# Two-block transformer on one core: gate and up of the feed-forward stages in seven products of quadrants instead of eight, down in five passes laid between the units

## The chip, the core and the metric

The kernel runs on one core of a Trainium2 chip. The metric is the device time of one execution in microseconds; the kernel before has a median of 3131.32 us over three runs (3129.34 to 3133.84).

Engines: TensorE (PE, matmuls; PEld its weight loads), VectorE (DVE), ScalarE (ACT), GpSimd (POOL), and SyncE (SP), which here issues the DMAs.

## The reference

512 tokens of width 1024 pass through one attention block (three attention branches, a linear recurrence, an output projection, a feed-forward stage) and then two layers of feed-forward stage, mixing stage (four kinds of attention over quarters of the width), feed-forward stage and final norm. A feed-forward stage is

```python
D_FF = -(-8 * D_MODEL // 768) * 256          # 2816

def rms_norm(x, g):
    y = xf * lax.rsqrt(jnp.mean(xf * xf, axis=-1, keepdims=True) + EPS)
    return (y * g.astype(jnp.float32)).astype(x.dtype)

def swiglu(h, w_gate, w_up, w_down):
    return (jax.nn.silu(h @ w_gate) * (h @ w_up)) @ w_down
```

so five times in the program: h = norm(x); x = x + c * swiglu(h), with c = 1 in stage 0 and 0.5 in stages 1 to 4. In order: attention block, output projection, stage 0, stage 1, mixing, stage 2, final norm, stage 3, mixing, stage 4, final norm.

## The kernel before, in words

Activations lie transposed: 8 tiles of 128 (width) by 512 (tokens). Every factor of a product is split in a high and a low part of the reduced type fp32r, and a product is three matmuls, high x high, low x high and high x low (`feat`, L142 to L144).

*Weights.* `stream` loads a block in pieces of 128x1024 (512 KB, L118, two buffers "raw" that all stages share), ScalarE makes the high part (L125) and VectorE or GpSimd the low part (L127), in halves of 512.

*A feed-forward stage* (`ffn`). Eleven units: each streams two weight blocks (gate, up; 8 k-tiles by 256 columns), multiplies them into two banks of 128x512 each, scales by the norm's broadcast factor rB (L521, L527), applies Silu (L522), multiplies (L528) and splits the result in fh and fl (L211 on ScalarE, L212 on VectorE). Then down: four blocks of 22 k-tiles, each adding two finished tiles into xT (L537, L539).

*Norm.* The factor of a token, 1/sqrt(mean x^2), is applied behind the matmul, so the next stage's matmuls need only xh and xl, the tile times the norm's gain. For each finished tile of xT, `norm_sq` squares it on ScalarE (L223) and sums on GpSimd (L225), and `norm_split` makes xh (L229, ScalarE) and xl (L230, VectorE). When all eight are done, `norm_r` reduces over partitions on PE (L195, `tokred`), makes the power (L186 VectorE, L188 GpSimd), and broadcasts on PE (L204, `bcast`) with a copy on ScalarE to rB (L207). `final_norm` does this with a second sum and also scales all of xT (L610).

*Order.* Instructions are put in order per engine by a scheduler, by priority: a `high_priority` block with a larger offset is drawn further ahead. Each engine runs its own queue in that order and waits on semaphores. Buffers come from pools; a pool closed at the end of a stage gives its memory to the pool opened next.

Of the kernel before, what the change touches and what calls it, by code (L numbers as in the profile page):

```python
# [84 lines left out]
class Kern:  # L85
# [419 lines left out]
    def ffn(self, f, half, norm):  # L505

        tc, nc, I = self.tc, self.nc, self.I
        V, S, G = nc.vector, nc.scalar, nc.gpsimd
        xh, xl, rB, xT = self.xh, self.xl, self.rB, self.xT
        ks = [(k, k) for k in range(8)]  # L510
        with tc.tile_pool(name="ph_f", bufs=1) as pf:
            self.pf = pf
            fh = [pf.tile([128, n, T], FR, name=f"fh{i}") for i, n in enumerate((8, 8, 6))]
            fl = [pf.tile([128, n, T], FR, name=f"fl{i}") for i, n in enumerate((8, 8, 6))]
            for j in range(11):
                wg = self.stream(I["w_g"][f, j], 8, 256)
                wu = self.stream(I["w_u"][f, j], 8, 256)
                z = [pf.tile([128, T], FT, tag="z", name="z", bufs=3) for m in range(2)]
                ps = self.feat2(wg, ks, lambda k: xh[:, k], lambda k: xl[:, k])
                for m in range(2):  # L520
                    V.tensor_mul(z[m], ps[m], rB)  # L521
                    S.activation(z[m], z[m], AF.Silu)  # L522
                ps = self.feat2(wu, ks, lambda k: xh[:, k], lambda k: xl[:, k])
                for m in range(2):
                    k = 2 * j + m
                    u = pf.tile([128, T], FT, tag="u", name="u", bufs=2)
                    V.tensor_mul(u, ps[m], rB)  # L527
                    V.tensor_mul(u, u, z[m])  # L528
                    self.split(fh[k // 8][:, k % 8], fl[k // 8][:, k % 8], u)
            for j in range(4):  # L530
                w = self.stream(I["w_d"][f, j], 22, 256)
                ps = self.feat2(w, [(k, k) for k in range(22)], lambda k: fh[k // 8][:, k % 8],
                                lambda k: fl[k // 8][:, k % 8])
                for m in range(2):
                    k = 2 * j + m
                    if half is None:
                        V.tensor_add(xT[:, k], ps[m], xT[:, k])  # L537
                    else:
                        V.scalar_tensor_tensor(xT[:, k], ps[m], half, xT[:, k], op0=OP.mult, op1=OP.add)  # L539
                    norm[0](k)  # L540
# [21 lines left out]
    def final_norm(self, l):  # L562
# [12 lines left out]
        def tile_done(k):  # L575
# [15 lines left out]
            g = gg[:, k:k + 1]  # L591
            S.activation(xh[:, k, :], xk, AF.Copy, scale=g)
            V.scalar_tensor_tensor(xl[:, k, :], xk, g, xh[:, k, :].bitcast(FT), op0=OP.mult, op1=OP.subtract)

        def finish():
            rf = self.rstd(self.tokred(acc, self.ones, 1), 1024, 4, "rt")
            if not last:
# [6 lines left out]
                self.xh, self.xl = xh, xl  # L604
            rB = self.bcast(rf, self.pf, "rF")
# [10 lines left out]
    def mix(self, px, l, norm):  # L616
# [253 lines left out]
        def diff():  # L870
# [29 lines left out]
            def head(h):  # L900
# [31 lines left out]
                def soft(qb):  # L932
# [4 lines left out]
                    for m in range(2):  # L937
# [88 lines left out]
        def na():  # L1026
# [26 lines left out]
            def head(h):  # L1053
# [21 lines left out]
                def soft(cb):  # L1075
# [584 lines left out]
def host(inputs):  # L1660
# [94 lines left out]
    for i, n in enumerate(("w_g", "w_u", "w_d")):  # L1755
        A[n] = np.stack([blocks(f[i], 256) for f in ff])
# [55 lines left out]
```

## Time and profile before

| | |
|---|---|
| median of three runs | 3131.32 us |
| the profiled execution | 3131.08 us, span 3129.3 us, mean granted clock 0.986 |
| PE busy | 3026.2 us, 97%, 15289 matmuls |
| VectorE, ScalarE, GpSimd busy | 55%, 44%, 24% |
| DMA over the span | 88 GB/s |

A window row gives for a stretch the busy time of an engine with the count of its instructions, the clock that was granted to PE (1.00 is 2.4 GHz, 0.50 is 1.2 GHz) and what the DMAs moved. Durations of matmuls overlap, so the step from one start to the next is the cost of one. In a timeline row the bracket at the end is the idle time of the engine before the instruction and what ended it.

### The profile page before, as it was taken

How to read it: one execution, taken by the hardware profiler on the slowest of the kernel's cores; microseconds unless marked ns; L12 is line 12 of the kernel's file. 1: busy time of each engine (PE TensorE's matmuls, PEld its weight loads, DVE VectorE, ACT ScalarE, POOL GpSimd, SP SyncE). 2: the span in 40 equal slices, each digit the busy share in tenths (PEclk: the TensorE clock that was granted, in tenths of full speed). 3: DMA queues.
4: the chain of work that ended last, by engine and by line, in shares of the span. 5: the costliest groups of instructions: out<-in, count | busy, mean ns of one | idle time of the engine just before them, and what ended most of it. 6: DMA issues, size and time to landing. Idle time of an engine off the chain costs nothing.

```text
span 3129.3 us, 41188 instructions
## 1 busy us (share of the span) xinstructions
PE 3026.2 (97%) x15289; PEld 2544.2 (81%) x15289; DVE 1718.7 (55%) x3144; ACT 1390.1 (44%) x2707; POOL 763.6 (24%) x722
## 2 busy tenths in 40 slices
PE   7999999999999999999989999999999998999998
PEld 6888777878888888889877888888888987778886
DVE  7676775444444444336787544355443488665433
ACT  4577774233333333236675333333332577543322
POOL 3466640010000000028863000010000878210000
PEclk9999999999999999999999999999999998999998
DMA  4211112343333233333211333323333321123332
GB/s 143 96 60 60 55 35 77 112 130 95 95 98 98 95 100 96 95 111 107 72 38 41 101 95 99 98 88 98 99 95 97 111 89 47 41 88 94 96 100 81
DMA packets 105266, 275.82 MB, mean 88 GB/s; under 512 B 27172, under 2 KB 36900, under 8 KB 104904
## 3 DMA queue, kind: packets, MB, share of 16 engines
q1 hardware_dynamic: 105064, 273.18, 28.3%
q8 instruction: 120, 1.97, 0.3%
q14 instruction: 82, 0.67, 0.1%
HBM read 268.93 MB, written 6.80 MB: 88 GB/s over the span
## 4 chain that ended last, share of the span: by engine, by line
PE 71%; issue 13%; DVE 7%; POOL 4%; ACT 2%; DMA 1%; SPq 0%; DVEq 0%; POOLq 0%; ACTq 0%
PE ps_mm L142 8%; PE ps_mm L144 8%; PE ps_mm L143 8%; PE ps_s L143 6%; PE ps_s L144 6%; PE ps_s L142 6%; PE ps_t L144 6%; PE ps_t L143 6%; PE ps_t L142 6%; PE ps_mm L172 2%; PE ps_mm L173 2%; PE ps_mm L174 2%; POOL lo L127 1%; PE ps_t L1579 1%; DVE PTl L212 1%
## 5 line engine op out<-in xcount | busy, mean ns | idle before, releaser
L125 ACT ACTIVATE hi<-raw 128x512 fp32r<-128x512 f32 (+2 forms) x952 | 593.7, 626 | 1353.2 <-PE ps_s L143 406.2
L127 DVE TENSOR_TENSOR lo<-raw,hi 128x512 fp32r<-128x512 f32 x782 | 547.5, 702 | 931.3 <-ACT hi L125 920.5
L225 POOL TENSOR_TENSOR acc<-acc,sq 128x512 f32<-128x512 f32 x49 | 74.4, 1518 | 1052.0 <-issue 525.7
L142 PE MATMUL ps_mm<-xh,hi 128*128 128x512 f32 (+1 forms) x792 | 311.2, 393 | 2.6 <-ACT hi L125 2.2
L144 PE MATMUL ps_mm<-xh,lo 128*128 128x512 f32 (+1 forms) x792 | 309.6, 392 | 3.1 <-POOL lo L127 3.1
L143 PE MATMUL ps_mm<-xl,hi 128*128 128x512 f32 (+1 forms) x792 | 310.0, 391 | 0.0
L142 PE MATMUL ps_s<-xh,hi 128*128 128x512 f32 x656 | 253.2, 391 | 7.9 <-ACT hi L125 7.8
L143 PE MATMUL ps_s<-xl,hi 128*128 128x512 f32 x656 | 257.5, 393 | 3.4 <-DVE xl L230 2.9
L172 PE MATMUL ps_mm<-hi,xh 128*128 128x256 f32 (+1 forms) x896 | 255.1, 288 | 2.3 <-ACT tk L651 1.0
L144 PE MATMUL ps_s<-xh,lo 128*128 128x512 f32 x656 | 256.2, 391 | 0.0
L127 POOL TENSOR_TENSOR lo<-raw,hi 128x512 fp32r<-128x512 f32 (+2 forms) x170 | 226.8, 1342 | 117.3 <-ACT hi L125 111.8
L173 PE MATMUL ps_mm<-lo,xh 128*128 128x256 f32 (+1 forms) x896 | 254.5, 286 | 0.1
L174 PE MATMUL ps_mm<-hi,xl 128*128 128x256 f32 (+1 forms) x896 | 252.6, 285 | 0.1
L142 PE MATMUL ps_t<-xh,hi 128*128 128x512 f32 x608 | 237.1, 390 | 0.0
L143 PE MATMUL ps_t<-xl,hi 128*128 128x512 f32 x608 | 236.9, 390 | 0.0
L144 PE MATMUL ps_t<-xh,lo 128*128 128x512 f32 x608 | 236.2, 390 | 0.6 <-DVE lo L127 0.5
L144 PEld LDWEIGHTS ps_mm<-xh,lo 128*128 128x128 f32 (+1 forms) x792 | 148.6, 188 | 35.3 <-POOL lo L127 4.1
L142 PEld LDWEIGHTS ps_mm<-xh,hi 128*128 128x128 f32 (+1 forms) x792 | 148.7, 188 | 34.3 <-ACT hi L125 2.5
L172 PEld LDWEIGHTS ps_mm<-hi,xh 128*128 128x128 f32 x896 | 171.1, 192 | 4.9 <-ACT tk L651 1.3
L173 PEld LDWEIGHTS ps_mm<-lo,xh 128*128 128x128 f32 x896 | 171.9, 192 | 2.2 <-POOL lo L127 0.7
L143 PEld LDWEIGHTS ps_mm<-xl,hi 128*128 128x128 f32 (+1 forms) x792 | 148.8, 188 | 30.5
L174 PEld LDWEIGHTS ps_mm<-hi,xl 128*128 128x128 f32 x896 | 171.2, 192 | 1.9 <-DVE xl L230 0.5
(527 smaller groups left out, 6654.9 us busy)
## 6 DMA issues: line engine op xcount, KB each, us to landing
raw<-in_w_g SPq DMA_DIRECT2D x110, 512.0 KB
raw<-in_w_u SPq DMA_DIRECT2D x110, 512.0 KB
raw<-in_w_d SPq DMA_DIRECT2D x108, 512.0 KB
raw<-in_w_o SPq DMA_DIRECT2D x24, 512.0 KB
raw<-in_w_c SPq DMA_DIRECT2D x16, 512.0 KB
raw<-in_w_m SPq DMA_DIRECT2D x16, 512.0 KB
raw<-in_w_a SPq DMA_DIRECT2D x12, 512.0 KB
raw<-in_w_d SPq DMA_DIRECT2D x20, 256.0 KB
```

The source lines that it names most:

```text
L125: nc.scalar.activation(hi[:, :c], x, AF.Copy)
L127: eng.tensor_tensor(lo[:, :c], x, hi[:, :c].bitcast(FT), op=OP.subtract)
L142: mm(ps, wh, mh(km), start=s, stop=False)
L143: mm(ps, wh, ml(km), start=False, stop=False)
L144: mm(ps, wl, mh(km), start=False, stop=e)
L172: mm(out[tb], h, wh, start=k == 0 and tb % 2 == 0, stop=False)
L173: mm(out[tb], h, wl, start=False, stop=False)
L174: mm(out[tb], o, wh, start=False, stop=k == K - 1 and tb % 2 == 1)
L212: self.nc.vector.tensor_sub(lo, src, hi.bitcast(FT))
L225: nc.gpsimd.tensor_tensor(acc, acc, sq, op=OP.add)
L1579: PE.transpose(tps[:, (qb - kb) * 128:(qb - kb + 1) * 128], P[qb][:, kb * 128:kb * 128 + 128], ident)
```

## The change

Gate and up of a unit form a matrix of two by two quadrants (k-tiles even and odd; gate and up) and the activations one of two by two (k-tiles even and odd; tokens 0 to 255 and 256 to 511). Seven products of sums of quadrants take the place of eight (Winograd's form of Strassen's scheme). `combine` makes from each finished pair of tiles of x the seven right factors, split in high and low; in a unit, GpSimd makes four sums of weight tiles (L571), ScalarE and VectorE split seven weight tiles of 128x1024 (L578, L579), PE runs seven products of 24 matmuls of 256 columns, and VectorE, ScalarE and GpSimd add the seven results up to gate and up (L619 to L647) ahead of the scaling and Silu in `act` (L596 to L598). Down runs in five passes over 4, 4, 4, 4 and 6 k-tiles; the first four lie between products of units 2, 4, 6, 8 and later ones, each pass adding into xT (L668). The weights of gate and up lie in a new order in the inputs, four tiles A0 to A3 of 128x1024 per unit; A0, A2, A3 come into four buffers "raw2" of the stage's own pool, A1 into the shared "raw". The mixing stage has some tiles moved into the memory that holds the combinations otherwise.

```diff
+    def combine(self, k, xk, g, xc):
+        V, S = self.nc.vector, self.nc.scalar
+        p = k // 2
+        if k % 2 == 0:
+            xc["x"] = self.t4("x")
+            if "hi" not in xc:
+                xc["hi"], xc["lo"] = ((self.xp.tile([128, 4, 4, 256], FR, tag="x" + n, name="x" + n),
+                                       self.x3.tile([128, 4, 3, 256], FR, tag="x3" + n, name="x3" + n)) for n in "hl")
+        x = xc["x"]
+        hi, lo = xc["hi"], xc["lo"]
+        S.activation(x[:, 2 * (k % 2):2 * (k % 2) + 2], xk.rearrange("p (a b) -> p a b", a=2), AF.Copy, scale=g)
+        if k % 2 == 0:
+            self.split(hi[0][:, p, 0], lo[0][:, p, 0], x[:, 0])
+            return
+        self.split(hi[0][:, p, 1:3], lo[0][:, p, 1:3], x[:, 2:4])
+        t = self.t4("t")
+        V.tensor_sub(t[:, 0], x[:, 1], x[:, 0])
+        V.tensor_sub(t[:, 1], x[:, 3], t[:, 0])
+        V.tensor_sub(t[:, 2], x[:, 3], x[:, 1])
+        V.tensor_sub(t[:, 3], x[:, 2], t[:, 1])
+        self.split(hi[0][:, p, 3], lo[0][:, p, 3], t[:, 0])
+        self.split(hi[1][:, p], lo[1][:, p], t[:, 1:4])
+    def norm_c(self, gname, g0):
+        acc, xc, xT = self.new_acc(), {}, self.xT
+        def tile_done(k):
+            self.combine(k, xT[:, k], self.col(gname, g0 + k), xc)
+            self.norm_sq(xT[:, k], k, acc)
+        def finish():
+            self.xc = xc["hi"], xc["lo"]
             self.r, self.rB = self.norm_r(acc)
         return tile_done, finish
...
@@ -504,40 +545,151 @@
     def ffn(self, f, half, norm):
         tc, nc, I = self.tc, self.nc, self.I
...
+        V, S, G, mm = nc.vector, nc.scalar, nc.gpsimd, nc.tensor.matmul
+        rB, xT = self.rB, self.xT
         with tc.tile_pool(name="ph_f", bufs=1) as pf:
             self.pf = pf
...
+            self.t4 = lambda n: pf.tile([128, 4, 256], FT, tag="c", name=n, bufs=3)
+            xh, xl = ([lambda p, c=c, x=x: x[c // 4][:, p, c % 4] for c in range(7)] for x in self.xc)
+            rT = rB.rearrange("p (t b) -> p t b", t=2)[:, :, None, :].to_broadcast([128, 2, 2, 256])
+            fh, fl = {}, {}
+            nbank = [0]
+            def load(u, i):
+                pool, tag, n = (self.wp, "raw", 2) if i == 1 else (pf, "raw2", 4)
+                t = pool.tile([128, 2 * T], FT, tag=tag, name=f"A{i}", bufs=n)
+                with tc.high_priority(offset=6000):
+                    nc.sync.dma_start(t, I["w_gu"][f, u, i])
+                return t
+            def add(a, b, op=OP.subtract):
+                t = pf.tile([128, 2 * T], FT, tag="S", name="S", bufs=3)
+                with tc.high_priority(offset=3000):
+                    G.tensor_tensor(t, a, b, op=op)
+                return t
+            def prod(x, c, ranges=((0, 4),)):
+                h, o = (pf.tile([128, 2 * T], FR, tag=n, name=n, bufs=3) for n in ("wh", "wl"))
+                with tc.high_priority(offset=3000):
+                    S.activation(h, x, AF.Copy)
+                    V.tensor_sub(o, x, h.bitcast(FT))
+                nbank[0] += 1
+                ps = self.bank(("mm", "s")[nbank[0] % 2])
+                for a, b in ranges:
+                    for i in range(2):
+                        out = ps[:, i * 256:i * 256 + 256]
+                        for p in range(a, b):
+                            sl = slice((4 * i + p) * 128, (4 * i + p) * 128 + 128)
+                            mm(out, h[:, sl], xh[c](p), start=i == 0 and p == 0, stop=False)
+                            mm(out, h[:, sl], xl[c](p), start=False, stop=False)
+                            mm(out, o[:, sl], xh[c](p), start=False, stop=i == 1 and p == 3)
+                    yield
+                return ps.rearrange("p (a b) -> p a b", a=2)
+            def act(u, j, c, eng):
+                k = 2 * u + j
+                eng.tensor_tensor(c, c, rT, op=OP.mult)
+                S.activation(c[:, :, 0], c[:, :, 0], AF.Silu)
+                V.tensor_mul(c[:, :, 0], c[:, :, 0], c[:, :, 1])
+                h, o = (pf.tile([128, T], FR, tag=n, name=n, bufs=8) for n in ("fh", "fl"))
+                self.split(*(x.rearrange("p (a b) -> p a b", a=2) for x in (h, o)), c[:, :, 0])
+                fh[k], fl[k] = h, o
+            def soon():
+                return tc.high_priority(offset=1000)
+            def unit(u):
+                a11, a21, a22 = load(u, 0), load(u, 2), load(u, 3)
+                s1 = add(a21, a22, OP.add)
+                s2 = add(s1, a11)
+                r = ((0, 3), (3, 4)) if u == 0 else ((0, 4),)
+                heads = [prod(x, c, r) for x, c in ((a11, 0), (s1, 3), (s2, 4))]
+                c1, c2 = (pf.tile([128, 2, 2, 256], FT, tag="c", name="c", bufs=3) for _ in range(2))
+                if u == 0:
+                    for g in heads:
+                        next(g)
+                ps = whole(heads[0])
+                with soon():
+                    S.copy(c1[:, 0], ps)
+                yield
+                ps = whole(heads[1])
+                with soon():
+                    S.copy(c2[:, 1], ps)
+                yield
+                ps = whole(heads[2])
+                with soon():
+                    V.tensor_add(c1[:, 1], ps, c1[:, 0])
+                yield
+                a12 = load(u, 1)
+                ps = whole(prod(a12, 1))
+                with soon():
+                    V.tensor_add(c1[:, 0], ps, c1[:, 0])
+                yield
+                ps = whole(prod(add(a11, a21), 5))
+                with soon():
+                    V.tensor_add(c2[:, 0], ps, c1[:, 1])
+                    G.tensor_tensor(c1[:, 1], c1[:, 1], c2[:, 1], op=OP.add)
+                    G.tensor_tensor(c2[:, 1], c2[:, 1], c2[:, 0], op=OP.add)
+                yield
+                ps = whole(prod(add(a12, s2), 2))
+                with soon():
+                    V.tensor_add(c1[:, 1], ps, c1[:, 1])
+                    act(u, 0, c1, G)
+                yield
+                ps = whole(prod(a22, 6))
+                with soon():
+                    V.tensor_add(c2[:, 0], ps, c2[:, 0])
+                    act(u, 1, c2, G if 2 <= u < 10 else V)
+                yield
+            def down(part, last):
+                n = len(part)
+                w, banks = {}, {}
+                def run(j, a, b, tag="t"):
+                    if j not in w:
+                        w[j] = self.stream(I["w_d"][f, j][:, part[0] * 256:(part[-1] + 1) * 256], n, 256)
+                        banks[j] = [self.bank(tag) for _ in range(2)]
+                    for i in range(a, b):
+                        for m in range(2):
+                            self.feat(banks[j][m], lambda k: pick(w[j](k), m), [(i, part[i])], lambda k: fh[k],
+                                      lambda k: fl[k], start=i == 0, stop=i == n - 1)
+                    if b < n:
+                        return
+                    for m in range(2):
+                        k = 2 * j + m
+                        V.scalar_tensor_tensor(xT[:, k], banks[j][m], 1.0 if half is None else half, xT[:, k],
+                                               op0=OP.mult, op1=OP.add)
+                        if last:
+                            norm[0](k)
+                if not last:
+                    for j in range(4):
+                        run(j, 0, n)
+                        yield
+                    return
+                run(0, 0, 4)
+                yield
+                run(1, 0, 4, "mm")
+                run(2, 0, 4, "s")
+                for j in range(3):
+                    run(j, 4, n)
+                run(3, 0, n)
+            d = iter(())
+            for u in range(11):
+                if u % 2 == 0 and u:
+                    d = down(list(range(2 * u - 4, 2 * u + (0 if u < 10 else 2))), u == 10)
+                for i, _ in enumerate(unit(u)):
+                    if i in ((2, 6) if u < 10 else (2,)):
+                        next(d, None)
+            whole(d)
             norm[1]()
```

In `final_norm` the two splits are replaced by `self.combine(k, xk, gg[:, k:k + 1], xc)`, the second sum lies in a buffer "S", and the broadcast rF in a buffer "raw2".

PE before, from the end of stage 0's down (where stage 1's matmuls already stand in front): ps_t and ps_mm are banks, xh and xl the normed activations, hi and lo the weights.

```order
4961 L142 MATMUL ps_t_9669<-xh_7062,hi_9638 128x512
4962 L143 MATMUL ps_t_9669<-xl_7063,hi_9638 128x512
4963 L144 MATMUL ps_t_9669<-xh_7062,lo_9639 128x512
4964 L195 MATMUL ps_n_9597<-ones_77,acc_7064 128x1 x4
4965 L142 MATMUL ps_t_9668<-xh_7062,hi_9642 128x512
4966 L143 MATMUL ps_t_9668<-xl_7063,hi_9642 128x512
4967 L144 MATMUL ps_t_9668<-xh_7062,lo_9643 128x512
...
4990 L143 MATMUL ps_mm_9722<-xl_7063,hi_9652 128x512
4991 L204 MATMUL ps_n_9606<-ident_75,rt_9604 128x128 x4
4992 L144 MATMUL ps_mm_9722<-xh_7062,lo_9653 128x512
```

L195 and L204 lie between the next stage's own matmuls, 26 of them apart.

PE now, the same place: fh and fl are the gated activations of stage 0, xh and xl now the combinations of stage 1, wh and wl its weight tile.

```order
5717 L142 MATMUL ps_t_10669<-fh_10453,hi_10664 128x512
5718 L143 MATMUL ps_t_10669<-fl_10454,hi_10664 128x512
5719 L144 MATMUL ps_t_10669<-fh_10453,lo_10665 128x512
5720 L195 MATMUL ps_n_10730<-ones_77,acc_7119 128x1 x4
5721 L204 MATMUL ps_n_10739<-ident_75,rt_10737 128x128 x4
5722 L587 MATMUL ps_s_10769<-xh_10555,wh_10765 128x256
5723 L588 MATMUL ps_s_10769<-xl_10557,wh_10765 128x256
5724 L589 MATMUL ps_s_10769<-xh_10555,wl_10766 128x256
```

L195 and L204 have the last matmul of stage 0 directly ahead of them and the first product of stage 1 directly behind.

SP before, with what each load waits for (a name is an engine or DMA queue whose semaphore is awaited), between stages 0 and 1:

```order
188 L118 DMA raw<-in_w_d 128x1024 [waits DMAHW5_49,DVE_49]
189 L118 DMA raw<-in_w_d 128x512 [waits DMAHW6_49,DVE_49]
190 L118 DMA raw<-in_w_g 128x1024 [waits DMAHW7_49,DVE_49]
191 L118 DMA raw<-in_w_g 128x1024 [waits DMAHW0_49,DVE_49]
192 L118 DMA raw<-in_w_u 128x1024 [waits DMAHW1_49,DVE_49]
```

The loads of w_g and w_u wait for a DMA queue and VectorE, as all loads of the stage before, which share the two buffers.

SP now, the same place; the three rows from A_10753 on are A0, A2 and A3 of stage 1's unit 0, the two ahead of them A1 of units 0 and 1:

```order
188 L118 DMA raw<-in_w_d 128x1024 [waits DMAHW7_49,DMAHW5_49,DVE_49]
189 L118 DMA raw<-in_w_d 128x512 [waits DMAHW6_49,DVE_49]
190 L565 DMA A_10855<-in_w_gu 128x1024 [waits DMAHW7_49,DVE_49]
191 L565 DMA A_11099<-in_w_gu 128x1024 [waits DMAHW0_49,DVE_49]
192 L565 DMA A_10753<-in_w_gu 128x1024 [waits DVE_49,PE_49,Pool_49]
193 L565 DMA A_10755<-in_w_gu 128x1024
194 L565 DMA A_10757<-in_w_gu 128x1024
```

A0 waits for VectorE, PE and GpSimd, and A2 and A3 stand behind it.

VectorE now, the same place, cut: x3h and x3l hold three of the seven combinations, t their sums, ps_n_10730 the bank of L195, wl_10766 the low part of A0's tile.

```order
1286 L668 SCALAR_TENSOR_TENSOR xT_6694<-ps_t_10668,xT_6694 128x512
1287 L389 TENSOR_TENSOR t_10640<-x_10629,t_10640 128x256
1288 L212 TENSOR_TENSOR x3l_10558<-t_10604,x3h_10556 128x768
1289 L668 SCALAR_TENSOR_TENSOR xT_6694<-ps_t_10669,xT_6694 128x512
...
1294 L386 TENSOR_TENSOR t_10718<-x_10707 128x256
...
1298 L387 TENSOR_TENSOR t_10718<-x_10707,t_10718 128x256
...
1300 L389 TENSOR_TENSOR t_10718<-x_10707,t_10718 128x256
1301 L186 TENSOR_SCALAR nm_10735<-ps_n_10730 128x4
1302 L212 TENSOR_TENSOR x3l_10558<-t_10718,x3h_10556 128x768
1303 L579 TENSOR_TENSOR wl_10766<-A0_10753,wh_10765 128x1024
1304 L579 TENSOR_TENSOR wl_10789<-S_10759,wh_10788 128x1024
```

The last split into x3l stands behind L186, and the first low part of a weight tile behind that split.

## Rows read from the trace of the kernel before

**Rows 1.** Page, part 1: busy time, share of the span and instructions of each engine

```profile
PE 3026.2 (97%) x15289; PEld 2544.2 (81%) x15289; DVE 1718.7 (55%) x3144; ACT 1390.1 (44%) x2707; POOL 763.6 (24%) x722
```

**Rows 2.** Windows, PE: length, busy (matmuls started), granted clock, DMA share, GB/s

```profile
800.00:900.00 100.00, 100.00 (x443) 1.00 0.32 100
1030.00:1040.00 10.00, 10.00 (x48) 1.00 0.23 76
1700.00:1710.00 10.00, 8.03 (x27) 0.66 0.04 18
1710.00:1720.00 10.00, 9.22 (x38) 1.00 0.16 53
1700.00:1707.00 7.00, 5.60 (x18) 0.53 0.06 25
```

**Rows 3.** Timeline, PE, 1410 to 1415 us: start, us, engine, line, op

```profile
1409.79 0.28 PE L174 MATMUL ps_mm<-hi,xl 128*128 128x256 f32 x1
1409.91 0.28 PE L172 MATMUL ps_mm<-hi,xh 128*128 128x256 f32 x1
...
1414.11 0.28 PE L173 MATMUL ps_mm<-lo,xh 128*128 128x256 f32 x1
```

**Rows 4.** Groups by line and shape: busy us, mean ns of one; idle before

```profile
L1471 DVE TENSOR_TENSOR tq<-tq,rq 128x1024 f32<-128x1024 f32 x4 | 5.1, 1284 | 0.8 <-POOL rq L188 0.8
L212 DVE TENSOR_TENSOR fl<-u,fh 128x512 fp32r<-128x512 f32 x110 | 75.4, 686 | 0.0
L212 DVE TENSOR_TENSOR PTl<-ps_t,PTh 128x256 fp32r<-128x256 f32 x32 | 13.4, 418 | 14.9 <-ACT PTh L211 14.9
L610 DVE SCALAR_TENSOR_TENSOR xT<-xT,cols,rF 128x512 f32<-128x512 f32 x13 | 11.9, 985 | 4.3 <-ACT rF L207 4.3
L493 ACT ACTIVATE gz<-gz 128x1024 f32<-128x1024 f32 x4 | 4.3, 1063 | 0.0
L501 POOL TENSOR_TENSOR yT<-gz,yT 128x1024 f32<-128x1024 f32 x4 | 10.1, 2528 | 0.0
L225 POOL TENSOR_TENSOR acc<-acc,sq 128x512 f32<-128x512 f32 x49 | 74.4, 1518 | 1052.0 <-issue 525.7 <-ACT sq L223 524.6
L188 POOL TENSOR_TENSOR rt<-nm,mhalf 128x4 f32<-128x4 f32 x10 | 10.6, 1057 | 388.4 <-DVE nm L186 388.4
```

**Rows 5.** Timeline, SP's queue, 972 to 978 us

```profile
973.33 0.33 SPq L118 DMA_DIRECT2D raw<-in_w_d  x1
```

**Rows 6.** Windows around that load: length, granted clock, DMA share, GB/s

```profile
972.00:974.20 2.20, 1.00 0.00 0
974.30:976.70 2.40, 1.00 0.73 217
976.70:979.00 2.30, 1.00 0.04 7
```

**Rows 7.** Timeline, GpSimd and VectorE in stage 0's down, behind two finished tiles

```profile
973.08 3.08 POOL L225 TENSOR_TENSOR acc<-acc,sq 128x512 f32<-128x512 f32 x2 [27.50 <-ACT sq L223]
973.59 3.12 DVE L230 SCALAR_TENSOR_TENSOR xl<-xT,cols,xh 128x512 fp32r<-128x512 f32 x2 [0.28 <-ACT xh L229]
```

**Rows 8.** Timeline, start of stage 2: ACT, DVE, PE, SP's queue, ACT

```profile
1700.89 0.58 ACT L207 COPY rB<-ps_n 128x512 f32<-128x512 f32 x1 [3.29 <-PE ps_n L204]
1701.51 1.29 DVE L865 TENSOR_TENSOR sqp<-ps_mm,rB 128x512 f32<-128x512 f32 x2 [3.11 <-ACT rB L207]
1702.71 1.28 DVE L866 TENSOR_TENSOR xT<-sqp,xT 128x512 f32<-128x512 f32 x2
1705.71 1.78 DVE L230 SCALAR_TENSOR_TENSOR xl<-xT,cols,xh 128x512 fp32r<-128x512 f32 x1
1707.41 0.63 PE L142 MATMUL ps_s<-xh,hi 128*128 128x512 f32 x2
1721.79 3.97 SPq L118 DMA_DIRECT2D raw<-in_w_g  x2
1725.68 0.63 ACT L125 ACTIVATE hi<-raw 128x512 fp32r<-128x512 f32 x1 [3.57 <-DMA raw<-in_w_g]
```

More of the change, by code (lines that the diff above doesn't have):

```diff
@@ L341, in block1 @@
                 self.skews(pk)
-            self.outproj(I["w_o"], mh, ml, self.norm("norm2", 0))
+            with tc.tile_pool(name="ph_o", bufs=1) as po:
+                self.t4 = lambda n: po.tile([128, 4, 256], FT, tag=n, name=n, bufs=2)
+                self.outproj(I["w_o"], mh, ml, self.norm_c("norm2", 0))
         self.dump("x1", xT)
-        self.ffn(0, None, self.norm("ffn1", 0))
+        self.ffn(0, None, self.norm_c("ffn1", 0))
         self.dump("x2", xT)
@@ L507, in ffn @@
         tc, nc, I = self.tc, self.nc, self.I
-        V, S, G = nc.vector, nc.scalar, nc.gpsimd
-        xh, xl, rB, xT = self.xh, self.xl, self.rB, self.xT
-        ks = [(k, k) for k in range(8)]
+        V, S, G, mm = nc.vector, nc.scalar, nc.gpsimd, nc.tensor.matmul
+        rB, xT = self.rB, self.xT
         with tc.tile_pool(name="ph_f", bufs=1) as pf:
             self.pf = pf
[L513 to L540, printed above, removed]
@@ L549, in block2 @@
             self.dump(f"xf1_{l}", xT)
-            norm = self.norm("ffn2", 8 * l)
+            norm = self.norm_c("ffn2", 8 * l)
             self.wide = False
@@ L590, in tile_done @@
                 G.tensor_tensor(acc2[0], acc2[0], sq, op=OP.add)
-            g = gg[:, k:k + 1]
-            S.activation(xh[:, k, :], xk, AF.Copy, scale=g)
-            V.scalar_tensor_tensor(xl[:, k, :], xk, g, xh[:, k, :].bitcast(FT), op0=OP.mult, op1=OP.subtract)
+            self.combine(k, xk, gg[:, k:k + 1], xc)
         def finish():
@@ L603, in finish @@
                 self.r, self.rB = r, self.bcast(r)
[L604 to L605 removed]
+                self.xc = xc["hi"], xc["lo"]
+            rB = self.bcast(rf, self.pf, "raw2", 4)
             for k in range(8):
@@ L630, in hot, with slot @@
             return tc.high_priority(offset=1000)
+        x3 = [self.x3.tile([128, 6, T], FT, tag=n, name="box3") for n in ("x3h", "x3l")]
+        slots = {"P": [x3[0][:, i] for i in range(6)] + [x3[1][:, i] for i in range(2)],
+                 "P1": [x3[1][:, i] for i in (2, 3)], "sqp": [x3[1][:, i] for i in (4, 5)]}
+        def slot(n):
+            slots[n].append(slots[n].pop(0))
+            return slots[n][-1]
+        self.t4 = lambda n: tl({"x": "tq", "t": "tk"}[n], [128, 4, 256], FT, 2, name=n)
         rows = tl("rows2", [128, ROWS["_2"]])
@@ L1754, in host @@
             ff.append(tuple(x[f"{n}_w_{m}_2"][i] for m in ("gate", "up", "down")))
-    for i, n in enumerate(("w_g", "w_u", "w_d")):
-        A[n] = np.stack([blocks(f[i], 256) for f in ff])
+    A["w_d"] = np.stack([blocks(f[2], 256) for f in ff])
+    A["w_gu"] = np.stack([np.stack(f[:2]).reshape(2, 4, 2, 128, 11, 2, 128).transpose(4, 5, 2, 3, 0, 1, 6)
+                          .reshape(11, 4, 128, 1024) for f in ff])
     A["rows2"] = np.stack([np.concatenate([x["mla_q_norm_2"][l][64:], x["mla_k_norm_2"][l][64:], x["gqa_q_norm_2"][l],
```

20 lines of the change are left out of this document (11 added, 9 removed).

## The prediction

> **What bounds the kernel now.** I read the page's first part first: PE is busy 97% of the span, every other engine 55% or less [rows 1]. Then the windows of PE, to see where the missing share lies. Inside a feed-forward stage there is none: 443 matmuls of 512 columns in 100 us at the full granted clock (1.00, the 2.4 GHz level), so one per 226 ns [rows 2]. Where stage 1 begins (1030 to 1040 us) PE is busy all ten microseconds too. Only the start behind a mixing stage shows a dent: 8.03 of 10 us at a clock of 0.66, then 9.22 [rows 2]. So the kernel is a chain of matmuls that is fed without a break, and any change is worth what it does to PE: columns times cadence, plus holes. I therefore price the matmuls first and then look for holes that the new order opens.
>
> **Matmuls removed and added.** A stage's gate and up were 11 units x 2 x 8 k x 2 m x 3 = 1056 matmuls of 512 columns: 1056 x 0.226 = 238.7 us. Now 11 units x 7 products x 24 = 1848 of 256 columns. Matmuls of that width run in this program too: from 1409.79 to 1414.11 us there are 36 steps, 4.32 / 36 = 0.120 us each [rows 3]. That gives 1848 x 0.120 = 221.8 us, so 16.9 us less per stage and 84.5 us less over five; the nominal eighth (29.8 us a stage) shrinks because two half-width matmuls cost 0.240 where one of full width cost 0.226. Down keeps its 528 matmuls. Matmul by matmul the stream is the same in kind (each with its own weight load), so I take the row's 0.120.
>
> The Trainium skill speaks against that row: "TensorE: Matmul & The Clock Gate", section "Wait — 56ns, not 53.3ns?", gives start to start as N / 2.4 GHz plus about 2.5 ns, which would be 109.2 ns at 256 columns and 215.7 ns at 512. The traced rows, 120 and 226 ns, are both about 10 ns longer, so the trace does not agree; by the page the new stage would take 201.8 us and the total would be about 100 us lower (a rival below).
>
> **Work beside the matmuls, inside the units.** A product takes 24 x 0.120 = 2.88 us, a unit 20.2 us, and with two pieces of down (5.42 us each) 31.0 us. Per unit ScalarE copies seven 128x1024 tiles (1.06 us each [rows 4]) and VectorE subtracts seven (1.28), both well under 31 us. GpSimd gets four adds of 128x1024 (2.53 us [rows 4]), two of 512 (1.52) and one or two multiplies of 1024: about 16 us. GpSimd and VectorE hinder each other: a VectorE operation on two SBUF tiles that meets a GpSimd add waits for it. Two such operations took 3.12 us beside two adds [rows 7], where alone they take 0.69 each [rows 4]. Counting for both engines only what must be exclusive I estimate 15.9 us of GpSimd and 12 us of VectorE, 27.9 of 31.0 us: it fits from unit 2 on, with preparation running ahead through three buffers. In units 0 and 1 there is no down to lie under, and the sum is 24.5 us against 20.2. What is late there is the tail (multiply, split), not the next product, so I take 2 us per stage, 10 us in all; the bounds are 0 (all deferred) and 2 x 4.3 x 5 = 43 us.
>
> **The starts of the five stages.** This is the term that decides. Before, the weights of the next stage were loaded, copied and multiplied while the last norm was still being made: at stage 1 the norm's reduction (L195) and broadcast (L204) lie among the next stage's own matmuls, and PE has no hole [rows 2]. The changed order has neither: on PE, L195 and L204 stand directly between the last matmul of one stage and the first of the next, and on SP the load of A0 of unit 0 waits for VectorE, PE and GpSimd, since the pool of its buffer is opened anew where the buffers of the finished stage lay. The VectorE instruction it waits for is the last split of the combinations (L212 into x3l); A2 and A3 are queued behind it on SP. So from the last matmul (T0) PE stands through: the tail of the combination, the load, the copy, and the first sums.
>
> Load and after, equal for all five: a 512 KB load issued at 973.33 [rows 5] moves between 974.3 and 976.7 us (2.40 x 217 GB/s = 521 KB) and nothing after [rows 6]: 3.4 us. Beside it stands the start behind the mixing stage, where the load was issued at 1721.79 and its copy began at 1725.68, 3.9 us [rows 8]. ScalarE's copy adds 1.1 [rows 4]; then the first product can run. The second and third need A2 and A3, that is two more transfers of 2.4 us, two GpSimd adds of 2.5 us in a row, a copy and a subtraction: the third ends about 18 us after the issue, where without waits it would end at 3.4 + 1.1 + 8.6 = 13.1; with part of it under the products I take 4.3 us. After such a hole the granted clock is low: 0.53 over 1700 to 1707 us, where PE had waited before [rows 2], so mostly the 1.2 GHz level. There some 3 us of matmuls cost 1.5 more. Fixed sum: 3.4 + 1.1 + 4.3 + 1.5 = 10.3 us; bounds 8.5 and 12.
>
> The tails, T0 to the issue. Combining a pair of tiles is on VectorE four subtractions of 256 (0.42), splits of 256, 512, 256 (0.42, 0.69, 0.42) and 768 (0.96, between the rows of 512 and 1024): 4.2 us, about 3.6 back to back, against two L230 before, 1.4 at the 0.69 of such an operation [rows 4].
> - Stage 0 (after the output projection): two adds, the ScalarE scale, one pair and one or two waits for GpSimd's sums: 8 us (6.5 to 10).
> - Stage 1: down's last pass ends six tiles within 8.1 us and two 8.1 us later, so VectorE has some 3.4 us of older pairs left at T0, plus the last pair and the waits: 11 us (8 to 14).
> - Stage 3: as stage 1 with more sums (13), then the reduction, two powers (1.06 [rows 4]) and the broadcast beside it, and eight scalings L610 of 0.985 = 7.9 [rows 4], for the load waits for the eighth: 21 us (14 to 24).
> - Stages 2 and 4 (after mixing): all eight tiles end at once. From the copy of the broadcast at 1700.89, VectorE's 16 operations at 0.60 (pairs of L865 and L866 start 1.20 apart) need 9.6 us, four pairs 14.4, five or six waits of 1.1 behind GpSimd (a L230 of 1.78 [rows 8]) some 6, start 0.6: the load is issued 30.6 us after the copy. Before, the next stage's matmuls ran from 1707.41, 6.5 us after it [rows 8]. Difference 24.1 us (18 to 29) each.
>
> Sum: 5 x 10.3 + 8 + 11 + 21 + 2 x 24.1 = 139.7 us; by the bounds about 108 to 166.
>
> **The rest.** The mixing stages keep their operations (tiles change place only), and the end of the kernel keeps its chain of norm and scalings; 0, and I allow 10 us to either side. From the profiled execution: 3131.1 - 84.5 + 10 + 139.7 = 3196 us. It lies 0.2 us under the median of the three runs, so nothing is to be converted. By the bounds: 3131 - 84.5 + 108 = 3155 to 3131 - 84.5 + 43 + 166 = 3256.
>
> **Rivals.**
> - The starts are covered (other side). Place: the five starts; price: 17 us each is the point, 84.5 / 5, at which gain and holes cancel. If the loads don't wait as the order says and only the first sums do, the term is 5 x 4.3 = 22 us: 3131 - 84.5 + 22 + 10 = 3078. For it: before shows no hole at these places. Against: the load, copy and tail follow each other by data and by buffer, and the fixed part alone is 10 us. 7%.
> - A 256-column stream runs nearer to half of a 512. Two matmuls in a row hold the same weights here; at 113 ns (half of 226) the stages take 208.8 us, 65 us less in all: 3131, no change; 3%. At the 109.2 ns of the page named above it is 20 us a stage more, 3096; against it stand 36 steps of 0.120 [rows 3]. 5%.
> - The port of GpSimd and VectorE bounds units 0 and 1, or more: each unit waits its 4.3 us, 3196 + 33 = 3229, and with steady units late as well beyond 3240. For it: 24.5 against 20.2; against: the late part is not on PE's path. 20%.
> - The holes are short: tails at their lower bounds, no waits for GpSimd: about 3155. 15%.
> - The forecast, 50%.
>
> **How the numbers follow.** Likeliest: 3196 us. Its own range, holes from 120 to 155 us, is 3175 to 3215. The range of eight in ten takes in the short holes and most of the port's case, and leaves the covered starts and the fast stream out below: 3138 to 3245. A difference under 0.2% (6 us) can't be told from none. Faster: 7 + 5 and little of the rest, 0.12; same, 0.04; slower, 0.84.
>
> **What would show it.** Right: in the windows, matmuls of 256 columns 0.120 us apart and none missing in units 3 to 9; five holes on PE, two near 35 us behind the mixing stages and three of 15 to 30, ended by ScalarE's copy L578 behind a DMA of A0; SP's wait at that load ended by VectorE's L212 (stage 3: L759); a clock near 0.5 just after. Wrong: A0 landed before the last matmul of the stage before; waits of PE on L578 or L579 spread over all units (the port); a cadence under 0.115.

## The result and the profile after

3315.07 us (median of 4 runs, 3310.73 to 3319.41) against 3132.43 before: ratio 1.0584, interval 1.0566 to 1.0603. Slower, as forecast, but by 183 us where 65 were forecast; the time lies outside the range of 3138 to 3245.

The page's first part of the changed kernel answers to [rows 1]:

```profile
PE 3008.3 (91%) x19249; PEld 2706.5 (82%) x19249; DVE 2630.8 (79%) x3439; ACT 1593.5 (48%) x2842; POOL 1882.4 (57%) x1147
```

PE's busy time fell by 18 us, VectorE rose from 55% to 79%, GpSimd from 24% to 57%. A window inside stage 0's units answers to [rows 2] (length; then PE, PEld, VectorE, ScalarE, GpSimd busy with counts; clock, DMA share, GB/s):

```profile
860.00:960.00 100.00, 96.70 (x664) 89.48 (x663) 92.95 (x75) 39.05 (x52) 63.45 (x25) 1.00 0.31 102
```

PE is no longer full, and VectorE shows 93%. Its own work is less: at the steps between its rows where nothing interferes (1.13 us for 1024 elements, 0.6 for 512) a steady unit, 24 operations, has 7 x 1.13 + 17 x 0.6, some 18 us, an estimate. Nine of the 17 read one input from PSUM, the banks that PE writes (names with ps); the other fifteen operations read two tiles in SBUF. The timeline of the changed kernel in that window, VectorE ahead, GpSimd below:

```profile
864.01 0.69 DVE L642 TENSOR_TENSOR c<-ps_s,c 128x512 f32<-128x512 f32 x1 [1.19 <-POOL c L637]
866.37 0.68 DVE L647 TENSOR_TENSOR c<-ps_mm,c 128x512 f32<-128x512 f32 x1
869.70 2.89 DVE L598 TENSOR_TENSOR c<-c 128x512 f32<-128x512 f32 x1
872.52 2.89 DVE L127 TENSOR_TENSOR lo<-raw,hi 128x512 fp32r<-128x512 f32 x1
875.33 2.88 DVE L212 TENSOR_TENSOR fl<-c,fh 128x512 fp32r<-128x512 f32 x1
898.98 0.68 DVE L647 TENSOR_TENSOR c<-ps_s,c 128x512 f32<-128x512 f32 x1
...
865.31 3.38 POOL L596 TENSOR_TENSOR c<-c,rB 128x1024 f32<-128x1024 f32 x1
868.65 3.39 POOL L571 TENSOR_TENSOR S<-A,S 128x1024 f32<-128x1024 f32 x1
872.01 2.85 POOL L596 TENSOR_TENSOR c<-c,rB 128x1024 f32<-128x1024 f32 x1
874.81 2.86 POOL L571 TENSOR_TENSOR S<-A,A 128x1024 f32<-128x1024 f32 x1
```

L647 comes once per unit: 898.98 - 866.37 = 32.6 us a unit, where PE needs 31.0; from 713.34 to 740.89 us units 0 and 1 are 27.6 apart, where PE needs 20.2. Three 512-element operations of VectorE took 2.8 to 2.9 us each, one ending just behind each GpSimd operation: the two engines take turns, one instruction each. [Rows 7] showed it once; here it recurs in every steady unit.

L647, which reads PSUM, kept its 0.68 us inside GpSimd's L596. From 866.37 to 898.98 us VectorE is busy 30.3 of 32.6 us: 18 us of its own work, 12 us of waits behind GpSimd inside its operations; of the 2.3 us in which it is idle, 1.2 are the wait for GpSimd's L637 (as the first row shows for the unit before) and the rest waits for ScalarE. GpSimd is busy 21.0 us.

The groups of VectorE, changed kernel:

```profile
L579 DVE TENSOR_TENSOR wl<-S,wh 128x1024 fp32r<-128x1024 f32 x220 | 480.8, 2185 | 30.2 <-ACT wh L578 29.9
L212 DVE TENSOR_TENSOR fl<-c,fh 128x512 fp32r<-128x512 f32 x110 | 162.3, 1486 | 24.5 <-ACT fh L211 24.5
```

A split of a GpSimd sum takes 2185 ns, of fl 1486 where before it took 686 [rows 4].

The starts of stages 0, 1, 2, 3 and 4, PE of the changed kernel; the bracket is the idle time before the row:

```profile
675.19 1.87 PE L195 MATMUL ps_n<-ones,acc 128*128 128x1 f32 x8 [4.17 <-POOL acc L225]
682.82 0.58 PE L587 MATMUL ps_s<-xh,wh 128*128 128x256 f32 x1 [1.63 <-ACT wh L578]
1062.24 1.87 PE L195 MATMUL ps_n<-ones,acc 128*128 128x1 f32 x8 [9.39 <-POOL acc L225]
1072.18 0.58 PE L587 MATMUL ps_s<-xh,wh 128*128 128x256 f32 x1 [4.14 <-ACT wh L578]
1781.64 1.87 PE L195 MATMUL ps_n<-ones,acc 128*128 128x1 f32 x8 [21.59 <-POOL acc L225]
1792.10 0.58 PE L587 MATMUL ps_s<-xh,wh 128*128 128x256 f32 x1 [5.05 <-ACT wh L578]
2179.16 1.86 PE L195 MATMUL ps_n<-ones,acc 128*128 128x1 f32 x8 [16.31 <-DVE acc L731]
2200.92 0.58 PE L587 MATMUL ps_s<-xh,wh 128*128 128x256 f32 x1 [10.97 <-ACT wh L578]
2912.20 1.87 PE L195 MATMUL ps_n<-ones,acc 128*128 128x1 f32 x8 [23.79 <-POOL acc L225]
2922.86 0.58 PE L587 MATMUL ps_s<-xh,wh 128*128 128x256 f32 x1 [5.26 <-ACT wh L578]
```

The last matmul of a stage ended where the bracket of its L195 begins. From there to the first product (L587) it is 11.8, 19.3, 32.1, 38.1 and 34.5 us, 136 in all. Stage 2's start in detail (GpSimd, VectorE, SP's queue, ScalarE):

```profile
1772.78 8.81 POOL L225 TENSOR_TENSOR acc<-acc,sq 128x512 f32<-128x512 f32 x2 [3.38 <-ACT sq L223]
1778.45 0.68 DVE L212 TENSOR_TENSOR xl<-x,xh 128x512 fp32r<-128x512 f32 x1
1783.55 0.16 DVE L186 TENSOR_SCALAR nm<-ps_n 128x4 f32<-128x4 f32 x1 [4.42 <-PE ps_n L195]
1786.49 0.96 DVE L212 TENSOR_TENSOR x3l<-t,x3h 128x768 fp32r<-128x768 f32 x1 [0.91 <-ACT x3h L211]
1787.52 1.75 SPq L565 DMA_DIRECT2D A<-in_w_gu  x4
1790.99 1.06 ACT L578 ACTIVATE wh<-A 128x1024 fp32r<-128x1024 f32 x1 [3.32 <-DMA A<-in_w_gu]
```

The load of A0 is issued 0.1 us behind the last split into x3l (1786.49 + 0.96) and its copy starts 3.5 us later; the first product needs 1.1 more. At stage 3 the chain is another one (VectorE; the last split, then the eight scalings of the final norm):

```profile
2179.03 0.94 DVE L212 TENSOR_TENSOR x3l<-t,x3h 128x768 fp32r<-128x768 f32 x1
2190.61 5.39 DVE L759 SCALAR_TENSOR_TENSOR xT<-xT,cols,raw 128x512 f32<-128x512 f32 x8 [5.66 <-ACT raw L207]
```

From the last matmul (2162.85) the combinations take 17.1 us; then the norm's two reductions, powers and broadcasts stand alone for 10.6 us, the scalings take 5.4, and load and copy 4.9. The cadence at full clock, PE of the changed kernel, is 0.12 us, as in [rows 3]:

```profile
1797.41 0.28 PE L587 MATMUL ps_s<-xh,wh 128*128 128x256 f32 x1
1797.53 0.28 PE L588 MATMUL ps_s<-xl,wh 128*128 128x256 f32 x1
```

By the last matmuls of each stage: stages 0 to 4 became longer by 21, 29, 40, 45 and 41 us, the mixing stages by 3 and 5.

### The profile page after: what moved, and what is told of

It is laid out like the page before. It is cut to its first block, busy times and chain, and to the rows that moved or that the text cites. A ratio compares the mean times of both kernels' runs of the same rounds, so it can differ in the third digit from the quotient of the medians.

```text
span 3312.0 us, 49876 instructions
## 1 busy us (share of the span) xinstructions
PE 3008.3 (91%) x19249; PEld 2706.5 (82%) x19249; DVE 2630.8 (79%) x3439; ACT 1593.5 (48%) x2842; POOL 1882.4 (57%) x1147
## 4 chain that ended last, share of the span: by engine, by line
PE 44%; DVE 33%; issue 8%; POOL 6%; ACT 5%; DMA 3%; SPq 0%; DVEq 0%; POOLq 0%; ACTq 0%
DVE wl L579 8%; DVE lo L127 5%; DVE c L598 3%; PE ps_t L142 3%; DVE fl L212 3%; PE ps_t L144 3%; PE ps_t L143 3%; PE ps_mm L142 3%; PE ps_mm L144 3%; PE ps_mm L143 3%; POOL c L637 3%; DVE xT L668 2%; PE ps_mm L172 2%; PE ps_mm L174 2%; PE ps_mm L173 2%
## 5 line engine op out<-in xcount | busy, mean ns | idle before, releaser
L579 DVE TENSOR_TENSOR wl<-S,wh 128x1024 fp32r<-128x1024 f32 x220 | 480.8, 2185 | 30.2 <-ACT wh L578 29.9
L127 DVE TENSOR_TENSOR lo<-raw,hi 128x512 fp32r<-128x512 f32 (+1 forms) x342 | 379.0, 1115 | 118.2 <-ACT hi L125 117.9
L125 ACT ACTIVATE hi<-raw 128x512 fp32r<-128x512 f32 (+2 forms) x512 | 309.2, 617 | 284.1 <-PE ps_mm L143 68.8
L571 POOL TENSOR_TENSOR S<-A,A 128x1024 f32<-128x1024 f32 x110 | 312.1, 2837 | 129.0 <-DVE wl L579 70.4
L578 ACT ACTIVATE wh<-S 128x1024 fp32r<-128x1024 f32 x220 | 233.4, 1061 | 259.9 <-POOL c L637 87.6
L142 PE MATMUL ps_t<-fh,hi 128*128 128x512 f32 x760 | 299.3, 395 | 20.8 <-DVE xT L668 20.8
L571 POOL TENSOR_TENSOR S<-S,A 128x1024 f32<-128x1024 f32 x55 | 138.2, 2512 | 297.9 <-issue 297.1
L143 PE MATMUL ps_t<-fl,hi 128*128 128x512 f32 x760 | 297.1, 391 | 0.4 <-DVE fl L212 0.4
L144 PE MATMUL ps_t<-fh,lo 128*128 128x512 f32 x760 | 296.5, 390 | 0.0
L596 POOL TENSOR_TENSOR c<-c,rB 128x1024 f32<-128x1024 f32 x95 | 295.6, 3112 | 1.1 <-DVE c L642 1.1
L589 PE MATMUL ps_mm<-xh,wl 128*128 128x256 f32 x920 | 263.4, 286 | 11.4 <-DVE wl L579 11.4
L587 PE MATMUL ps_s<-xh,wh 128*128 128x256 f32 x840 | 245.4, 292 | 27.8 <-ACT wh L578 27.1
L579 DVE TENSOR_TENSOR wl<-A,wh 128x1024 fp32r<-128x1024 f32 x165 | 237.1, 1437 | 35.1 <-ACT wh L578 25.5
L587 PE MATMUL ps_mm<-xh,wh 128*128 128x256 f32 x920 | 262.6, 285 | 0.0
L578 ACT ACTIVATE wh<-A 128x1024 fp32r<-128x1024 f32 x165 | 173.6, 1055 | 178.5 <-PE ps_mm L588 85.0
```

The lines of the kernel that those rows point to most:

```text
L127: eng.tensor_tensor(lo[:, :c], x, hi[:, :c].bitcast(FT), op=OP.subtract)
L142: mm(ps, wh, mh(km), start=s, stop=False)
L143: mm(ps, wh, ml(km), start=False, stop=False)
L144: mm(ps, wl, mh(km), start=False, stop=e)
L571: G.tensor_tensor(t, a, b, op=op)
L578: S.activation(h, x, AF.Copy)
```

## The experiments

The theory after the result: in the units VectorE and GpSimd work one at a time (theory A), so 17.1 us of VectorE and 15.5 of GpSimd (six operations of 1024 at 2.25 and two of 512 at 1.0, estimates) make the 32.6. That this sum meets the period to a tenth is luck: by the counts above VectorE has some 18 us, GpSimd has 16.5 by its shortest steps in the trace (2.33 and 1.25 us), and VectorE's operations that read PSUM run beside GpSimd's. The expectations below use the sum as it was. Rivals: VectorE's queue is too long (B), or results come late through few buffers or a slow GpSimd (C).

**All unit work on VectorE.**

```diff
-                    G.tensor_tensor(t, a, b, op=op)
+                    V.tensor_tensor(t, a, b, op=op)
...
-                    G.tensor_tensor(c1[:, 1], c1[:, 1], c2[:, 1], op=OP.add)
+                    V.tensor_tensor(c1[:, 1], c1[:, 1], c2[:, 1], op=OP.add)
...
-                    act(u, 1, c2, G if 2 <= u < 10 else V)
+                    act(u, 1, c2, V)
```

> Every GpSimd operation of the units (four weight sums of 128x1024, L637, L638, the scaling L596) goes to VectorE. Theory A (the shared port): in a unit GpSimd and VectorE run as one engine, since every GpSimd operation stops VectorE's queue: 17.1 us of VectorE + 15.5 us of GpSimd = 32.6 us, the period measured for units 2 to 9, against 31.0 of PE. On VectorE alone the moved work takes 8 us (four sums and two scalings of 1.13, two of 0.6), the sum is 25 us in a steady unit and 21.5 in units 0 and 1: period 31.0 us (PE bounds) and 21.5 to 23 in units 0 and 1 (27.6 now), so 8 x 1.6 + 2 x 5 = 23 us less per stage, 115 in all: about 3200 us. Theory B (VectorE's queue itself, 93% busy, is too long): its 30.3 us become 38, the period too, 3315 + 5 x 8 x 6 = 3550 us or more. Theory C (the units are bound by latency through few buffers): no change beyond 1%, 3315.

3205.02 us, 1.0236 [1.0220, 1.0251] of before: 110 us less than the change. Its window and its L647 (units 0 to 2, and two of the steady ones):

```profile
860.00:960.00 100.00, 100.00 (x704) 94.10 (x703) 85.32 (x103) 41.49 (x54) 0.00 (x0) 1.00 0.32 98
```

```profile
704.17 0.70 DVE L647 TENSOR_TENSOR c<-ps_s,c 128x512 f32<-128x512 f32 x1
729.60 0.71 DVE L647 TENSOR_TENSOR c<-ps_mm,c 128x512 f32<-128x512 f32 x1
751.02 0.72 DVE L647 TENSOR_TENSOR c<-ps_s,c 128x512 f32<-128x512 f32 x1
842.90 0.68 DVE L647 TENSOR_TENSOR c<-ps_mm,c 128x512 f32<-128x512 f32 x1
873.98 0.69 DVE L647 TENSOR_TENSOR c<-ps_s,c 128x512 f32<-128x512 f32 x1
```

PE is full, the steady period is 31.1, the first two 25.4 and 21.4. VectorE does more and is busy less. Its groups, against those above:

```profile
L579 DVE TENSOR_TENSOR wl<-S,wh 128x1024 fp32r<-128x1024 f32 x220 | 268.9, 1224 | 28.3 <-ACT wh L578 24.9 <-PE ps_mm L589 0.4
```

The period came out as theory A said, the time 5 us above it. Theory B is out, and C as far as few buffers go, for their number is the same; that results came late from a slow GpSimd is not.

**Only the weight sums on VectorE.**

```diff
-                    G.tensor_tensor(t, a, b, op=op)
+                    V.tensor_tensor(t, a, b, op=op)
```

> Only the four weight sums (L571) go to VectorE; L637, L638 and the scalings stay on GpSimd. Theory A: VectorE 17.1 + 4.5 and GpSimd 6.8 make 28.4 us, below 31.0, so steady units run at 31.0 us, units 0 and 1 at about 23: 3205 us, nearly all of the gain of moving everything. Theory B: VectorE's queue longer by 4.5 us, period 35 to 37, 3430 us or more. Theory C: 3315.

3196.40 us, 1.0207 [1.0192, 1.0222]: the whole gain, and 9 us more. The difference is not in the units (294 us against 293 from the first L647 to the last) but in the two mixing stages (together 636 us against 656), which I did not follow up.

**GpSimd busy with work that nobody needs.** This tells the port from the wait for data.

```diff
                     V.tensor_tensor(t, a, b, op=op)
+                    for _ in range(2):
+                        G.tensor_tensor(pf.tile([128, T], FT, tag="S2", name="S2"), rB, rB, op=op)
```

> The kernel with the four weight sums on VectorE (3196 us), and GpSimd given as much work again that nobody needs: for each sum two subtractions of the tile rB from itself into a tile that is never read (about 8 x 1.3 = 10.4 us per unit). The output is the same. Nothing in the unit waits for them. Theory A (the port: each GpSimd operation stops VectorE's two-input operations): VectorE's 21.6 us and GpSimd's 6.8 + 10.4 us don't fit into 31.1 us side by side; the period of steady units becomes 34 to 39 us, the time 3350 to 3600 us. Rival (the units were long in the changed kernel because results came late from a slow GpSimd, that is by waiting for data): nothing waits for these results, period 31.1, 3196 us.

3458.01 us, 1.1041 [1.1021, 1.1061]. Nothing waits for these operations, so GpSimd ran through stage 0's stock by about 900 us; the run holds its own control, with the same 28 VectorE operations in a unit on either side. Windows with the idle work and behind it, then L649 (L647 of the other kernels) across the border:

```profile
820.00:900.00 80.00, 68.88 (x438) 63.56 (x438) 77.38 (x57) 25.57 (x35) 73.03 (x42) 0.93 0.28 83
940.00:1030.00 90.00, 90.00 (x624) 84.25 (x623) 84.31 (x83) 37.26 (x50) 28.82 (x12) 1.00 0.30 86
```

```profile
862.31 0.68 DVE L649 TENSOR_TENSOR c<-ps_s,c 128x512 f32<-128x512 f32 x1
903.35 0.68 DVE L649 TENSOR_TENSOR c<-ps_mm,c 128x512 f32<-128x512 f32 x1
934.21 0.68 DVE L649 TENSOR_TENSOR c<-ps_s,c 128x512 f32<-128x512 f32 x1
965.29 0.68 DVE L649 TENSOR_TENSOR c<-ps_mm,c 128x512 f32<-128x512 f32 x1
```

A unit of 41.0 us while GpSimd is 91% busy, 30.9 and 31.1 once the idle work is used up. VectorE is busy 97% of the first window, with operations drawn out, and 94% of the second. So the taking of turns is enough to lengthen a unit, with no data that come late. (In the changed kernel the 1.2 us per unit for L637 are a wait for data, a small part of what its units lose.) The Trainium skill, "SBUF — State Buffer", section "Who interferes with whom", says that a VectorE instruction with two SBUF inputs contends with a GpSimd instruction that reads SBUF, and calls the pair of ports that they share an exclusive lock. The trace of the changed kernel agrees: 2.8 us where 0.69 is the work, and L647, with one input in PSUM, at its 0.68 us beside L596.

**One pool over two stages.**

```diff
+        with tc.tile_pool(name="ph_f", bufs=1) as pf:
+            self.pf = pf
+            self.ffn(0, None, self.norm_c("ffn1", 0))
+            self.ffn(1, 0.5, self.norm("mix", 0))
...
-        with tc.tile_pool(name="ph_f", bufs=1) as pf:
-            self.pf = pf
+        if True:
+            pf = self.pf
```

> One pool of buffers is kept open over stages 0 and 1, and one over stages 2 and 3, instead of a new one per stage; nothing else. Then the weights of unit 0 of stage 1 are loaded, copied and split while stage 0's down still runs, and on PE about 57 products stand ahead of L195. Theory A (the load behind the closed pool is what the start of a stage waits for): of the 19.3 us from stage 0's last matmul to stage 1's first product nearly all go, and the two waits behind it shrink: 15 to 22 us less in stage 1; in stage 3 the order on PE did not change, 0 to 5 us; 3315 - 20 = 3295. Theory B (the norm's sums and the combinations bound the start whatever the weights do): the matmuls run out behind L195 and wait there, at most 4 us less, 3311.

3292.27 us, 1.0513 [1.0498, 1.0529], 23 less than the change. Stage 1 took 14 us less and stage 3 7 less; stage 0 took 3 more. SP's queue and PE at stage 1's start:

```profile
1019.46 0.33 SPq L567 DMA_DIRECT2D A<-in_w_gu  x1
1021.75 2.06 SPq L567 DMA_DIRECT2D A<-in_w_gu  x2
1056.06 0.39 PE L589 MATMUL ps_mm<-xh,wh 128*128 128x256 f32 x1 [0.97 <-ACT xh L211]
1059.16 0.58 PE L590 MATMUL ps_mm<-xl,wh 128*128 128x256 f32 x1 [2.71 <-DVE xl L212]
1062.70 0.58 PE L590 MATMUL ps_s<-x3l,wh 128*128 128x256 f32 x1 [1.12 <-DVE x3l L212]
```

The weights are requested at 1019 to 1022 us, before stage 0's last matmul; of the hole, waits of 1.0, 2.7 and 1.1 us for the combinations are left. The load behind the closed pool was the cause in stage 1. In stage 3 the norm's reductions, powers and broadcasts still stand between the last matmul and the first product, and 31 of the 38 us stay.

**Both edits.**

> Both edits, all unit work on VectorE and one pool per pair of stages. If the terms add: 3315 - 115 - 20 = 3180 us. If VectorE's longer queue delays the combinations at the start of stages, some of the second is lost: 3190 to 3200.

3188.38 us, 1.0186 [1.0169, 1.0203]: 127 less than the change; the terms add within 6 us.

**The norms' sums on VectorE as well.**

```diff
-            nc.gpsimd.tensor_tensor(acc, acc, sq, op=OP.add)
+            nc.vector.tensor_tensor(acc, acc, sq, op=OP.add)
```

> All unit work on VectorE and one pool per pair of stages (3188 us), and the seven sums of squares of a norm (L225) on VectorE too. At the starts of stages 2 and 4 PE waits 22 us at L195 for the last of these sums; in the changed kernel the last two took 8.8 us beside a dense run of VectorE's operations. Theory A (GpSimd is kept out by VectorE there): the sums cost 7 x 0.6 us on VectorE and the waits on both sides go, L195 starts 4 to 8 us earlier at stages 2 and 4, 1 to 2 at 0 and 1: 3170 to 3178. Rival (VectorE's queue alone bounds these starts): 4 us more on it at every start, 3195 to 3205.

3153.17 us, 1.0067 [1.0053, 1.0081]; 35 us less, where 10 to 18 were expected. VectorE, SP's queue and PE at stage 2:

```profile
1709.32 0.68 DVE L225 TENSOR_TENSOR acc<-acc,sq 128x512 f32<-128x512 f32 x1
1712.13 0.15 DVE L186 TENSOR_SCALAR nm<-ps_n 128x4 f32<-128x4 f32 x1
1712.28 1.75 SPq L567 DMA_DIRECT2D A<-in_w_gu  x4
1710.15 1.84 PE L195 MATMUL ps_n<-ones,acc 128*128 128x1 f32 x8 [20.79 <-DVE acc L225]
1717.34 0.58 PE L589 MATMUL ps_s<-xh,wh 128*128 128x256 f32 x1 [1.84 <-ACT wh L580]
```

The last two sums take 0.7 us each instead of 8.8 for the pair, and the gap of 4.4 us on VectorE is gone; PE's wait at L195 is still 20.8, so L195 did not start the 4 to 8 us earlier that were expected: VectorE is now dense up to the load. What fell is the time behind it: the first product of stage 2 stands 28.0 us behind the last matmul instead of 32.1. Stages 0 and 1 gave 6 us, 2 and 4 about 5 each, the output projection 5; some 14 us came in the mixing stages, whose order also moved, and that part is not explained.

**The seven products in stages 0 and 1 only**: the combinations and the new stage put into the kernel before, called for f = 0 and 1 in one pool, the rest as before.

> The seven products in stages 0 and 1 only, with one pool over both and the weight sums on VectorE; stages 2 to 4 and the mixing stages as in the kernel before. The starts behind mixing (about 33 us each) and before stage 3 (27) don't arise; what is left is the start of stage 0 (12 us and two waits) and units 0 and 1 of each stage against 33.8 us less on PE. In the kernel with both edits stages 0 and 1 took 712.8 us against 721.7 before: 3131 - 9 = 3122 us. If the first term of the theory (matmul columns at 0.120 us) were wrong: 3131 or more.

3134.57 us, 1.0010 [1.0001, 1.0019] of before, 13 us more than expected: stages 0 and 1 took 717 us against 722, and the mixing stage behind them 321 against 315.

> As the run with the seven products in stages 0 and 1 only, but all unit work on VectorE, none on GpSimd: 3122 us as well, 3118 if the remaining GpSimd operations (6.8 us per unit) still cost VectorE time in units 0 and 1.

3129.92 us, 0.9993 [0.9984, 1.0002]: no change, 8 us more than expected. Stages 0 and 1 took 714 us against 722, as expected, but the mixing stage behind them 320 against 315; why is not shown.

> The seven products in stages 0 and 1 only with all unit work on VectorE (3130 us), and the norms' sums of squares (L225) on VectorE in the whole program. In the run with both edits in all stages the sums brought 6 us for stages 0 and 1 and some 4 at the end of the output projection: 3120 us. If the sums bring something at every norm, also where the stages are as before: 3112. If VectorE is too full at the starts that are as before: 3130 or more.

3113.44 us, 0.9944 [0.9930, 0.9957]: faster than both kernels, than the one before by 18.6 us, and nearer to the 3112 of the sums' helping at every norm than to 3120. Stages 0 and 1 took 707 us.

> Control: the kernel before with nothing changed but the sums of squares (L225) on VectorE instead of GpSimd. Theory A (a sum on GpSimd costs VectorE more than it saves): the waits of 1.1 us behind sums at the starts of stages 2 and 4 go, PE's idle time there is 2 to 3 us each, so 3126 to 3131 us; the rest is hidden. Rival (the sums alone, without the seven products, gave what the sums gave in all stages, 35 us): 3100.

3123.77 us, 0.9975 [0.9966, 0.9984]: the sums alone give 8 us, 2 more than the range expected. Of the 18.6 us of the run with both, the seven products in two stages alone gave 2, not clear of noise; some 9 come only with the two together, and the runs don't show why.

## Why the prediction was wrong

- *Matmuls*: right. 0.120 us a step and no hole in PE where the port is free (all unit work on VectorE); the rival of a faster stream is out.
- *Units*: the step that failed. "What is late there is the tail (multiply, split), not the next product, so I take 2 us per stage, 10 us in all", and before it "27.9 of 31.0 us: it fits". From the first L647 of a stage to its last the changed kernel takes 312.4 us, with all unit work on VectorE 292.6: 99 us in five stages. The work that excludes the other engine was counted about right: in a steady unit VectorE's fifteen operations on two SBUF tiles make 12.7 us and GpSimd's eight 15.5 to 16.5, together 28 to 29. What was wrong is the overlap: I let all else of VectorE lie under GpSimd's operations. In the rows some 4 us of it do not, operations that read PSUM and waits for ScalarE at times when GpSimd has nothing running: 32.6 us. And the late work is on PE's path: over the program PE waited for low parts of weights (L579) 65 times, 62.9 us in all, and for L668 29 times, 20.8 us. Waits on L579 over all units were the sign that the prediction gave for the port. That rival, at 20%, had the mechanism, but I priced it too low at 3229 and more: taking the work off GpSimd gave back 110 to 119 us.
- *Starts*: right in place and cause, somewhat short in size: 136 us of holes up to the first product against 111 by my terms (8 + 11 + 21 + 2 x 24.1, and 4.5 each). Half of the difference is stage 3, 38.1 against 25.5: there I let the reductions, powers and broadcasts lie beside the combinations, at no cost, and they stood alone for 10.6 us behind them. Of stages 2 and 4, GpSimd's last two sums, 8.8 us, and VectorE's L186, which waited 4.4 us for them ahead of the last splits, were missing. The granted clock just after the holes was as forecast, 0.50 to 0.60 over the first 4 to 5 us (0.50 from 1792 to 1796).
- *The rest*: 0 forecast, 7.5 us measured in the mixing stages.
- Sum: -84.5 + 136 + 7.5 leaves 124 of the 183 us. The units take 99 of them, for which I had 10; some 25 are left for the first sums and the low clock after a hole, for which I had 29.

## What to carry to other kernels

Before you move elementwise work to GpSimd to relieve VectorE, add GpSimd's time to VectorE's two-input operations on SBUF tiles, and do not take it for granted that VectorE's other operations lie under GpSimd's: here 28 to 29 us of such work made a period of 32.6. The moved work can cost more than it frees. A scheme that saves matmuls pays only where its preparation hides, and the place to look is where one stage ends and the next needs weights: here a pool closed between two stages made stage 1 wait for its weights, 14 us. Seven products paid here in two of five stages, and only with the norms' sums on VectorE as well.

## What the runs showed of the hardware that was not expected

In the units GpSimd and VectorE alternate (three VectorE operations of 128x512 took 2.8 us each, 0.69 of it work, beside GpSimd's of 128x1024 in 2.9), but a dense run of two-input operations on VectorE, of 128x256 to 128x768, kept GpSimd out: two sums took 8.81 us from 1772.78, where such a sum took 1.5 on average before [rows 4], and ended at 1781.59, 2.5 us after VectorE had gone idle (1778.45 + 0.68). Stage 4 repeats it, with 8.81 us again. Which of the two patterns arises was not tried apart.
